# Hybrid decoder layer on one core: a third buffer for weights and their two parts, and the GLA diagonal moved into a score run

## The chip, the core and the metric

The kernel runs on one core of a Trainium2 chip. The metric is the device time of one execution in microseconds; the number given for a kernel is the median of its runs. Beside it there is a profile of one execution, taken by the hardware profiler. The engines of the core are TensorE (PE; its weight loads are PEld), VectorE (DVE), ScalarE (ACT), GpSimd (POOL) and SyncE (SP); SP, ACT and POOL also issue transfers (DMAs).

## The reference

One layer of a hybrid decoder over 16 meta tokens and 512 tokens (528 rows), width 2048, in float32. The normalised input goes through one projection of 7,585 columns; three token mixers share its columns, each on heads of its own; their outputs, gated, go through one output projection of 2048 x 2048, the input is added, and a last RMS norm follows.

```python
h = rms_norm(x, norm_w)
proj = h @ w_in
(dq, dk, dv, dz, db, da, gq, gk, gv, gz, gl, fq, fk, fv, fz, ff) = split_cols(proj)
...
o_dn = gated_delta_rule_chunked(q_dn, k_dn, v_dn, log_a, beta)      # 6 heads of 128
o_gla = gla_chunked(q, k, v, log_g)                                 # 5 heads, keys 64, values 128
o_fox = forgetting_attention(q, k, v, log_f)                        # 5 heads of 128
...
o = jnp.concatenate([o_dn, o_gla, o_fox], axis=-1)
return x + o @ w_out
```

The change touches the scores of GLA, linear attention with a decay for each key dimension. Within a chunk

```python
dec = jnp.exp(jnp.where(causal, g_c[:, :, :, None, :] - g_c[:, :, None, :, :], -jnp.inf))
attn = jnp.einsum('bhid,bhjd,bhijd->bhij', q_c, k_c, dec)
```

On the diagonal (i = j) the decay is 1, so the score there is the plain product of a token's query and its key.

## The kernel before

**Precision.** TensorE multiplies most operands as pairs: a float32 array is split into a high part, which ScalarE casts (`A.copy(hi, raw)`, L170), and a low part, the difference, which VectorE makes (L171). Each product then takes three matmuls: high by high, high by low, low by high.

**The weights.** A weight block is 128 columns of the input projection; its 2048 rows come as two halves of 128 x 1024 numbers (512 KB). `load_half` (L143) has SP load a half into a buffer `raw` (L147) and splits it into `whi` and `wlo`. The three kinds of buffer are tags (`raw`, `hi`, `lo`) of the pool `wp`, each with two buffers of 4 KB per partition. Where sums of weights are to be prepared, a copy from DRAM to DRAM (into `ti` or `tw`) is tied behind a raw load on SP's queue (L149), and POOL later adds to it by accumulating transfers (L490, L495). The split has high priority in the order of ScalarE and VectorE.

**The stages.** TensorE goes through the blocks in turn, with `inproj_part` (L238): two groups of 264 columns (all 528 rows) by 16 row tiles by 3, that is 96 matmuls a block, 48 a half; a block without meta tokens has 48 matmuls of 512 columns. First come four gate blocks (`dz`, L307) while the input itself arrives (`xs`, split into `xh` and `xl`) and ScalarE sums the squares of the token rows (`xt`, ten loads of up to 512 KB, L342 and L343, which go through the same tags `raw`, `hi` and `lo` in turn); then the delta-rule heads, the GLA gates, three GLA head pairs (heads 0 and 1, 2 and 3, and 4 alone), and the forgetting-attention heads, of which the later ones use pairs of blocks with seven products instead of eight (`inproj_pair`, L576: 24 matmuls a product). The output projection (L1426), with weights of 512 columns, and the last norm end the kernel.

**The order of the work.** The program is ordered ahead of time: each engine gets one list, from priorities and a simulated schedule. For single matmuls the place among those of the projection is written by hand: `PLACE` (L202) gives, for the first matmul into a named PSUM tile, a block and the number of that block's matmul behind which it shall stand. `"pss11": (('fv', 0), 26)` puts the first matmul of score run 1 of GLA pair 1 behind matmul 26 of block `fv` 0. A tile not in the table goes where the schedule puts it.

**GLA scores.** `gla_pair` (L981 on) computes the scores of a chunk by levels. For level s (64, 32, 16, 8, 4, 2, 1) the tokens are cut into blocks of 2s; queries of the second half of each block meet keys of the first half, both scaled by the decay to the boundary. VectorE subtracts (L1044, L1046), ScalarE takes the exponential (L1047), and VectorE scales keys and queries into `kq` (L1048, L1051). Two levels form a run, whose 64x64 matmuls (L1071, PSUM tiles `pss<pair><run>`, one per head) then stand together; a run's results are copied by ScalarE (levels 64 and 32) or by VectorE with a mask (`copy_predicated`, L1086) into `a64`, and from there by ScalarE into `at` (L1089), which the product with the values reads (`pgo`, L1139). Level 1 uses the unscaled keys.

The diagonal was done apart: POOL multiplies keys by queries (L1027), four matmuls per pair with a constant of two columns (`half_c`) sum over the key dimension of each head (`psd`, L1030), and VectorE spreads the column over the diagonal through a mask (L1032).

float32 operands that are not split take TensorE two instructions for each matmul in the profile, so a run of two levels and two heads shows as x64.

Of the kernel before, what the change touches and what calls it, by code (L numbers as in the profile page):

```python
# [8 lines left out]
F32 = mybir.dt.float32  # L9
F32R = mybir.dt.float32r  # L10
# [4 lines left out]
ALU = mybir.AluOpType  # L15
# [3 lines left out]
P = 128  # L19
D = 2048  # L20
KT = D // P
NM = 16
# [3 lines left out]
NB = S // P  # L26
# [56 lines left out]
def tile_hybrid_trunk(ctx, tc, xT, xtok, mtok, w_gate, w_in, w_out, w_dn, consts, lmask, fin_w, out, dbg=None):  # L83
    nc = tc.nc
# [3 lines left out]
    cst = pool("cst", 1)  # L88
    hp = pool("hp", 2 * KT)
    wp = pool("wp", 2)  # L90
# [3 lines left out]
    psm = pool("psm", 4, space=PSUM)  # L94
# [8 lines left out]
    V, A, G, PE = nc.vector, nc.scalar, nc.gpsimd, nc.tensor  # L103
# [10 lines left out]
    G.memset(ones, 1.0)  # L114
    eps_c = cst.tile([P, 1], F32, name="eps_c")
    G.memset(eps_c, EPS)
    half_c = cst.tile([P, 2], F32, name="half_c")
    G.memset(half_c, 0.0)
    for e in range(2):
        G.memset(half_c[64 * e : 64 * e + 64, e : e + 1], 1.0)  # L120
    zero_c = cst.tile([P, 1], F32, name="zero_c")
    G.memset(zero_c, 0.0)
    cpk = cst.tile([P, 101], F32, name="cpk")
# [19 lines left out]

    def load_half(src, name, raw=None):
        if raw is None:
            raw = wp.tile([P, 1024], F32, tag="raw", name=f"raw{name}")
        ring.append(nc.sync.dma_start(out=raw, in_=src).ins)  # L147
        if moves:
            x = nc.sync.dma_start(**moves.pop(0)).ins  # L149
            tc.add_manual_dep(x, ring[-1].name, mybir.DependencyInfo(  # L150
                mybir.DependencyClass.NoSync, mybir.DependencyReason.DATA), reason="ring")
            ring.append(x)
        hi = wp.tile([P, 1024], F32R, tag="hi", name=f"whi{name}")
        lo = wp.tile([P, 1024], F32R, tag="lo", name=f"wlo{name}")
        split(raw, hi, lo)
        due[0] += rate[0]
        while due[0] > 0 and chores:
            cost = next(chores[0], None)
            if cost is None:
                chores.pop(0)  # L160
            else:
                due[0] -= cost
        return hi, lo
# [34 lines left out]
    def part(name, n=512):  # L198
# [6 lines left out]
        "pss02": (('gk', 2), 26),  # L205
        "pss03": (('gk', 2), 46),
        "pg00": (('gk', 2), 72),
        "pss10": (('fk', 0), 92),
        "pss11": (('fv', 0), 26),
        "pss12": (('fv', 0), 54),  # L210
        "pss13": (('fv', 0), 78),
        "pg01": (('fq', 0), 8),
        "pss21": (('fk', 1), 60),
        "pss22": (('fk', 1), 84),
        "pgo2": (('pair', 0), 8),
    }

    def behind(mm, n):
# [118 lines left out]
    for b in range(5):  # L337
        r = NM if b == 4 else P
        for c in range(2):
            t = wp.tile([P, 1024], F32, tag=("raw", "hi", "lo")[(2 * b + c) % 3], name=f"xt{b}{c}")  # L340
            src = mtok if b == 4 else xtok[b * P : (b + 1) * P]
            nc.sync.dma_start(out=t[:r], in_=src[:, c * 1024 : (c + 1) * 1024])  # L342
            A.activation(t[:r], t[:r], AF.Square, accum_out=ssq[:r, b, c : c + 1])  # L343
# [11 lines left out]
    A.copy(rstd[:, :NM], pr[1][:, :NM])  # L355


    wgr = wp.tile([P, 1024], F32, tag="raw", name="rawgate")
    nc.sync.dma_start(out=wgr, in_=w_gate)
    wg = []  # L360
    for i, tag in enumerate(("hi", "lo")):
        w3 = wp.tile([P, 8, P], F32R, tag=tag, name=f"wg{i}")
        r3 = wgr[:, 512 * i : 512 * i + 512].rearrange("p (k c) -> p k c", c=64)
        A.copy(w3[:, :, 0:64], r3)
        V.tensor_tensor(out=w3[:, :, 64:], in0=r3, in1=w3[:, :, 0:64].bitcast(F32), op=ALU.subtract)
        wg.append(w3)
# [613 lines left out]
    def gla_pair(p):  # L980
# [41 lines left out]
        def masked(i, n):  # L1022
            return lmk[:, i, :].unsqueeze(1).to_broadcast([P, n, 64])


        prod = spare[:R]
        G.tensor_tensor(out=prod, in0=kT[:, NM:], in1=qT[:, NM:], op=ALU.mult)  # L1027
        psd = psm.tile([P, 512], F32, tag="m", name=f"psd{p}")
        for b in range(NB):
            PE.matmul(psd[:, b : b + NB * (ne - 1) + 1 : NB], prod[:, b * P : (b + 1) * P], half_c[:R, :ne],  # L1030
                      start=True, stop=True)
        V.copy_predicated(a64[:, :n_n], masked(5, n_n), psd[:, :n_n].unsqueeze(2).to_broadcast([P, n_n, 64]))  # L1032

        halves = lambda t_, s: t_.rearrange("p (n h s) -> p n h s", h=2, s=s)

        def scores(s, li):
# [14 lines left out]
            kqs.append(V.tensor_tensor(out=v4[:, :, 1, :], in0=qv[:, :, 1, :], in1=dv[:, :, 1, :], op=ALU.mult).ins)  # L1051
            return kq if s > 1 else kT[:, NM:], kq

        runs, li = ((64, 32), (16, 8), (4, 2), (1,)), 0
        for ri, run in enumerate(runs):
            ops = []
            for s in run:
                ops.append((s, *scores(s, li)))
                li += 1
            pss = [psm.tile([P, 512], F32, tag="m", name=f"pss{p}{ri}{e}") for e in range(ne)]  # L1060
            heads2 = [(e, pss[e], slice(64 * e, 64 * e + 64), slice(NB * e, NB * e + NB)) for e in range(ne)]
            c, got = 0, []
            for s, kx, qx in ops:
                n = s if s > 16 else 64
                for b in range(NB):
                    for r in range(P // (2 * n) if s > 16 else 2):
                        k0 = b * P + r * (2 * n if s > 16 else n)
                        q0 = k0 + n if s > 16 else k0
                        o0 = 2 * n * r if s > 16 else n * r
                        for e, ps, rr, en in heads2:  # L1070
                            mm = PE.matmul(ps[o0 : o0 + n, c + b * n : c + b * n + n], kx[rr, k0 : k0 + n],  # L1071
                                           qx[rr, q0 : q0 + n], start=True, stop=True)
                            place(f"pss{p}{ri}", mm)
                got.append((s, c, c + NB * n))
                c += NB * n
            for s, c0, c1 in got:
                for e, ps, rr, en in heads2:
                    pc = ps[:, c0:c1].rearrange("p (n c) -> p n c", n=NB)
                    if s == 64:
                        A.copy(at[0:64, en, 64:128], pc[0:64])  # L1080
                    elif s == 32:
                        for q in range(2):
                            sl = slice(64 * q, 64 * q + 32)
                            A.copy(a64[sl, en, 32:64], pc[sl])
                    else:
                        V.copy_predicated(a64[:, en], masked((16, 8, 4, 2, 1).index(s), NB), pc)  # L1086
        for q in range(2):
            sl = slice(64 * q, 64 * q + 64)
            A.copy(at[sl, :n_n, sl], a64[sl, :n_n])  # L1089
# [339 lines left out]
    halves = lambda w: [[t[:, j * 512 : (j + 1) * 512] for t in w] for j in range(2)]  # L1429

    def load_last(kp):
        raw = wp.tile([P, 1024], F32, tag="raw", name=f"rawl{kp}")
# [269 lines left out]
```

## Time and profile before

| | |
|---|---|
| median of 3 runs | 980.81 us (980.05 to 981.07) |
| the profiled execution: its time / its span | 981.26 us / 979.6 us |
| granted TensorE clock in it | 0.998 |
| TensorE / weight loads / VectorE / ScalarE / GpSimd busy | 967.9 / 890.6 / 674.9 / 477.0 / 229.7 us |
| transfers | 191.88 MB; SP's queue 152.63 MB, POOL's 31.66 MB |

The page gives, for each engine, the time in which it was busy, its share of the span and the number of instructions. A group of instructions is one line of the source, engine, operation and tiles, with the number of instructions, then busy time, mean length of one in ns, idle time of the engine just before them and what ended it. A wait reads "who <- for whom: us in total, times, longest". In a timeline each row has start, length, engine, line, operation, tiles written <- read, shape, count, and in brackets the idle time before. A table by stage gives for each stretch its length and then the busy time (and count) of PE, PEld, DVE, ACT and POOL, the granted clock, the share of the DMA engines and GB/s. Matmuls are pipelined: one is shown with its whole length, longer than the distance to the next.

### The profile page before, as it was taken

The numbers are of one execution on the slowest core, as the hardware profiler recorded it, in microseconds if no ns is written. First come the engines' busy times: TensorE is split into PE (matmuls) and PEld (weight loads), VectorE is DVE, ScalarE is ACT, GpSimd is POOL, SyncE is SP. The second block draws the span as 40 slices with busy tenths as digits, with TensorE's granted clock in tenths as the row PEclk, the third lists the DMA queues.
The fourth block names the chain that finished last, engine by engine and source line by source line (L and its number), as shares of the span: only waits on it lengthen the run. The fifth ranks groups of instructions, "written<-read, shape, count | busy, mean of one in ns | idle before, by whom it ended". The sixth has DMA issues, their size and how long they took to land.

```text
span 979.6 us, 19040 instructions
## 1 busy us (share of the span) xinstructions
PE 967.9 (99%) x7362; PEld 890.6 (91%) x7362; DVE 674.9 (69%) x1462; ACT 477.0 (49%) x1043; POOL 229.7 (23%) x251
## 2 busy tenths in 40 slices
PE   9999999999999999999999999999999999999996
PEld 7899999899999888899999889899999998888885
DVE  5468777876558885344685858766867768986664
ACT  7754433345356334344545545554555545544345
POOL 0032322232123234211213223232332120000023
PEclk9999999999999999999999999999999999999999
DMA  9835587987558787644647566678775478456534
GB/s 345 302 129 208 179 204 212 283 234 219 171 151 233 211 231 197 170 119 101 161 132 192 140 174 166 197 202 228 195 202 173 173 264 287 148 204 217 182 127 173
DMA packets 70336, 191.88 MB, mean 196 GB/s; under 512 B 14077, under 2 KB 17325, under 8 KB 69476
## 3 DMA queue, kind: packets, MB, share of 16 engines
q1 hardware_dynamic: 46048, 152.63, 44.7%
q0 software_dynamic: 15104, 31.66, 18.6%
q10 hardware_dynamic: 9092, 6.36, 2.3%
q8 instruction: 58, 0.95, 0.4%
q14 instruction: 34, 0.28, 0.1%
HBM read 179.93 MB, written 60.88 MB: 246 GB/s over the span
## 4 chain that ended last, share of the span: by engine, by line
PE 95%; DVE 2%; DMA 1%; issue 1%; ACT 0%; POOL 0%; SPq 0%; ACTq 0%; DVEq 0%
PE pp L238 46%; PE pp_a L576 8%; PE pq L1426 6%; PE pp L307 5%; PE pa L1426 3%; PE pt L1426 3%; PE ps L1426 3%; PE pp_b L576 2%; PE pp_d L576 2%; PE pp_c L576 2%; PE pr L1426 1%; PE pss L1071 1%; PE pfo L1301 1%; PE pgate L424 1%; DMA zd<-gqk 1%
## 5 line engine op out<-in xcount | busy, mean ns | idle before, releaser
L238 PE MATMUL pp<-xh,whi 128*128 128x264 f32 (+2 forms) x1120 | 270.3, 306 | 0.0
L238 PE MATMUL pp<-xh,wlo 128*128 128x264 f32 (+2 forms) x1120 | 268.9, 305 | 1.0 <-DVE wlo L171 1.0
L238 PE MATMUL pp<-xl,whi 128*128 128x264 f32 (+2 forms) x1120 | 269.7, 305 | 0.0
L170 ACT CAST whi<-raw 128x1024 fp32r<-128x1024 f32 x131 | 137.2, 1047 | 186.6 <-PE pp L238 115.4
L171 DVE TENSOR_TENSOR wlo<-raw,whi 128x1024 fp32r<-128x1024 f32 x131 | 162.3, 1239 | 53.3 <-ACT whi L170 46.4
L238 PEld LDWEIGHTS pp<-xh,wlo 128*128 128x128 f32 x1120 | 181.3, 189 | 9.5 <-DVE wlo L171 1.2
L238 PEld LDWEIGHTS pp<-xl,whi 128*128 128x128 f32 x1120 | 181.5, 189 | 8.8 <-issue 0.5
L238 PEld LDWEIGHTS pp<-xh,whi 128*128 128x128 f32 x1120 | 181.2, 188 | 8.8
L383 POOL TENSOR_SCALAR stc<-cv 128x528 f32<-128x528 f32 (+1 forms) x18 | 28.4, 1579 | 129.2 <-DVE cv L618 127.5
L618 DVE SCALAR_TENSOR_TENSOR cv<-pb,cpk,cv 128x528 f32<-128x528 f32 (+1 forms) x54 | 40.8, 756 | 0.8
L1455 POOL TENSOR_TENSOR acc<-acc,fw 128x512 f32<-128x512 f32 x4 | 6.1, 1552 | 138.4 <-DVE wll L171 138.4
L170 ACT CAST whis<-raws 128x1024 fp32r<-128x1024 f32 x20 | 20.7, 1049 | 28.2 <-PE pq L1426 12.2
L171 DVE TENSOR_TENSOR wlos<-raws,whis 128x1024 fp32r<-128x1024 f32 x20 | 24.2, 1223 | 14.9 <-ACT whis L170 14.8
L576 PE MATMUL pp_a<-t,whi 128*128 128x264 f32 (+1 forms) x224 | 29.3, 282 | 0.0
L576 PE MATMUL pp_a<-xl,whi 128*128 128x264 f32 x112 | 28.3, 287 | 0.0
L576 PE MATMUL pp_a<-xh,whi 128*128 128x264 f32 x112 | 28.1, 284 | 0.0
L576 PEld LDWEIGHTS pp_a<-t,whi 128*128 128x128 f32 x224 | 27.6, 188 | 0.0
L490 POOL DMA_DIRECT2D tw<-tw x16 | 13.4, 835 | 59.5 <-DVE wlo L171 30.2
L372 DVE TENSOR_TENSOR pb<-pp,rstd 128x264 f32<-128x264 f32 (+1 forms) x36 | 13.8, 424 | 19.5 <-PE pp L238 19.4
L383 POOL TENSOR_SCALAR stdz<-zdz 128x512 f32<-128x512 f32 x6 | 11.2, 1876 | 63.7 <-DVE zdz L401 55.3
L1426 PE MATMUL pq<-whia,a 128*128 128x512 f32 x80 | 25.5, 394 | 0.0
L1426 PE MATMUL pq<-whis,s 128*128 128x512 f32 x80 | 25.3, 394 | 0.0
(510 smaller groups left out, 2129.4 us busy)
## 6 DMA issues: line engine op xcount, KB each, us to landing
raw<-in_w_in SPq DMA_DIRECT2D x103, 512.0 KB, 3.9
ti<-in_w_in SPq DMA_DIRECT2D x28, 512.0 KB, 5.3
raw<-ti SPq DMA_DIRECT2D x28, 512.0 KB, 3.5
tw<-in_w_dn SPq DMA_DIRECT2D x20, 512.0 KB, 5.1
raws<-tw SPq DMA_DIRECT2D x15, 512.0 KB, 4.1
ti<-in_w_in POOLq DMA_DIRECT2D x14, 512.0 KB, 6.9
ti<-ti POOLq DMA_DIRECT2D x14, 512.0 KB, 6.5
tw<-in_w_dn POOLq DMA_DIRECT2D x10, 512.0 KB, 7.2
```

Of the source, the lines that this page charges most:

```text
L170: pace[0] = A.copy(hi, raw).ins
L171: pace[1] = V.tensor_tensor(out=lo, in0=raw, in1=hi.bitcast(F32), op=ALU.subtract).ins
L238: mm = PE.matmul(p_[:, :nt], wt[:, j * m : (j + 1) * m], xx[k][:, t0 : t0 + nt], start=(k == 0 and wt is hi and xx is xh), stop=(k == KT - ...
L307: mm = PE.matmul(ps[:, :S], wt[:, j * P : (j + 1) * P], xx[k][:, NM:T], start=(k == 0 and wt is hi and xx is xh), stop=(k == KT - 1 and wt ...
L372: V.tensor_tensor(out=o, in0=p_[rows], in1=rstd[rows, t0 : t0 + n], op=ALU.mult)
L383: maxes.append(G.tensor_scalar_max(t, src, LOW).ins)
L424: PE.matmul(pgate[a][:, :HT], wg[k // 8][:, k % 8, :], xx[k][:, a * HT : (a + 1) * HT], start=(k == 0 and xx is xh), stop=(k == KT - 1 and ...
L490: x = G.dma_start(out=out_[s], in_=in_[s], accum_op=ALU.add, max_dma_last_dim=2048)
L576: m = PE.matmul(p_[:, cols], wt[:, j * P : (j + 1) * P], xx[j][part_][:, cols], start=first and i == 0, stop=i == len(todo) - 1, skip_grou ...
L618: V.scalar_tensor_tensor(out=c, in0=pb[:, t0 + w : w + T], scalar=cwc[:, blk, w : w + 1], in1=c, op0=ALU.mult, op1=ALU.add)
L1071: mm = PE.matmul(ps[o0 : o0 + n, c + b * n : c + b * n + n], kx[rr, k0 : k0 + n], qx[rr, q0 : q0 + n], start=True, stop=True)
L1426: mm = PE.matmul(p_, o_[:, s], w_, start=(first and n == 0), stop=(last and n == 2), skip_group_check=True)
```

## The change

Four things change together.

1. The tags `raw`, `hi` and `lo` have three buffers each instead of two, for weights, the token rows, the gate weights and the last output weights alike.
2. The memory for that, 12 KB per partition, comes from the scratch of GpSimd's transfers: the program is built with 4,096 bytes per partition for it, where the default is 16,384.
3. The diagonal of the GLA scores is no longer computed apart. The last run of each pair, which held level 1 alone, gets a level 0: unscaled keys by unscaled queries in 64x64 blocks, one more half of the PSUM tiles that the run has; its results go through `copy_predicated` with the mask of the diagonal. The POOL product, `half_c` and the `psd` matmuls go.
4. In `PLACE` the score runs of pair 1 move back (run 0 from matmul 92 of `fk` 0 to matmul 4 of `fv` 0, which is 8 matmuls, run 1 by 12, run 2 by 6), run 0 and run 3 of pair 2 get a place, its runs 1 and 2 move back by 12 and 10, and its product with the values (`pgo2`) moves back by 16.

```diff
     def load_half(src, name, raw=None):
         if raw is None:
-            raw = wp.tile([P, 1024], F32, tag="raw", name=f"raw{name}")
+            raw = wp.tile([P, 1024], F32, tag="raw", bufs=3, name=f"raw{name}")
...
-        hi = wp.tile([P, 1024], F32R, tag="hi", name=f"whi{name}")
-        lo = wp.tile([P, 1024], F32R, tag="lo", name=f"wlo{name}")
+        hi = wp.tile([P, 1024], F32R, tag="hi", bufs=3, name=f"whi{name}")
+        lo = wp.tile([P, 1024], F32R, tag="lo", bufs=3, name=f"wlo{name}")
...
-        "pss10": (('fk', 0), 92),
-        "pss11": (('fv', 0), 26),
-        "pss12": (('fv', 0), 54),
+        "pss10": (('fv', 0), 4),
+        "pss11": (('fv', 0), 38),
+        "pss12": (('fv', 0), 60),
         "pss13": (('fv', 0), 78),
         "pg01": (('fq', 0), 8),
-        "pss21": (('fk', 1), 60),
-        "pss22": (('fk', 1), 84),
-        "pgo2": (('pair', 0), 8),
+        "pss20": (('fk', 1), 34),
+        "pss21": (('fk', 1), 72),
+        "pss22": (('fk', 1), 94),
+        "pss23": (('fq', 1), 10),
+        "pgo2": (('pair', 0), 24),
...
-            t = wp.tile([P, 1024], F32, tag=("raw", "hi", "lo")[(2 * b + c) % 3], name=f"xt{b}{c}")
+            t = wp.tile([P, 1024], F32, tag=("raw", "hi", "lo")[(2 * b + c) % 3], bufs=3, name=f"xt{b}{c}")
...
-        prod = spare[:R]
-        G.tensor_tensor(out=prod, in0=kT[:, NM:], in1=qT[:, NM:], op=ALU.mult)
-        psd = psm.tile([P, 512], F32, tag="m", name=f"psd{p}")
-        for b in range(NB):
-            PE.matmul(psd[:, b : b + NB * (ne - 1) + 1 : NB], prod[:, b * P : (b + 1) * P], half_c[:R, :ne],
-                      start=True, stop=True)
-        V.copy_predicated(a64[:, :n_n], masked(5, n_n), psd[:, :n_n].unsqueeze(2).to_broadcast([P, n_n, 64]))
...
-        runs, li = ((64, 32), (16, 8), (4, 2), (1,)), 0
+        runs, li = ((64, 32), (16, 8), (4, 2), (1, 0)), 0
...
-                ops.append((s, *scores(s, li)))
+                ops.append((s, *scores(s, li)) if s else (0, kT[:, NM:], qT[:, NM:]))
...
-                        V.copy_predicated(a64[:, en], masked((16, 8, 4, 2, 1).index(s), NB), pc)
+                        V.copy_predicated(a64[:, en], masked((16, 8, 4, 2, 1, 0).index(s), NB), pc)
...
-    nc = bacc.Bacc("TRN2", target_bir_lowering=False, num_devices=1)
+    nc = bacc.Bacc("TRN2", target_bir_lowering=False, num_devices=1, dynamic_dma_scratch_size=4096)
```

More of the change, by code (lines that the diff above doesn't have):

```diff
@@ L116, in tile_hybrid_trunk @@
     G.memset(eps_c, EPS)
[L117 to L120, printed above, removed]
     zero_c = cst.tile([P, 1], F32, name="zero_c")
@@ L355, in tile_hybrid_trunk @@
     A.copy(rstd[:, :NM], pr[1][:, :NM])
-    wgr = wp.tile([P, 1024], F32, tag="raw", name="rawgate")
+    wgr = wp.tile([P, 1024], F32, tag="raw", bufs=3, name="rawgate")
     nc.sync.dma_start(out=wgr, in_=w_gate)
@@ L361, in tile_hybrid_trunk @@
     for i, tag in enumerate(("hi", "lo")):
-        w3 = wp.tile([P, 8, P], F32R, tag=tag, name=f"wg{i}")
+        w3 = wp.tile([P, 8, P], F32R, tag=tag, bufs=3, name=f"wg{i}")
         r3 = wgr[:, 512 * i : 512 * i + 512].rearrange("p (k c) -> p k c", c=64)
@@ L1431, in load_last @@
     def load_last(kp):
-        raw = wp.tile([P, 1024], F32, tag="raw", name=f"rawl{kp}")
+        raw = wp.tile([P, 1024], F32, tag="raw", bufs=3, name=f"rawl{kp}")
         nc.sync.dma_start(out=raw, in_=w_out[3, kp])
```

## The prediction

> **What bounds the kernel now.** I read the head of the page first, then TensorE's waits, then the chain of waits in order of time (start, length, what).
>
> ```profile
> span 979.6 us, 19040 instructions
> PE 967.9 (99%) x7362; PEld 890.6 (91%) x7362; DVE 674.9 (69%) x1462; ACT 477.0 (49%) x1043; POOL 229.7 (23%) x251
> ...
> PE 95%; DVE 2%; DMA 1%; issue 1%; ACT 0%; POOL 0%; SPq 0%; ACTq 0%; DVEq 0%
> ```
>
> ```profile
> PE pss L1071 <- DVE kq L1051: 1.4, 2, 1.2
> PE warm L302 <- POOL ones L114: 1.2, 1, 1.2
> PE pp L238 <- DVE wlo L171: 1.0, 1, 1.0
> ```
>
> ```profile
> 563.00 1.09 PE pss L1071 x64
> ...
> 594.65 0.98 PE psd L1030 x8
> ...
> 612.80 1.08 PE pss L1071 x32
> ...
> 709.63 2.93 PE pp_a L576 x24
> ...
> 969.39 2.14 PE pz L1426 x18
> ```
>
> TensorE is busy for 967.9 of 979.6 us, so it is idle for 11.7. Its last matmul ends at 969.39 + 2.14 = 971.5, which leaves a tail of 8.1 us. The start takes 1.2 us, the wait for `ones`. The other 2.4 us are the two remaining rows of waits, 1.4 and 1.0. Between start and tail there is next to nothing to win from idle time; what is left is the number and the length of the matmuls. Their pace: 24 of 264 columns take 2.93 us, 0.122 us each.
>
> Where do those 2.4 us lie? The timeline of one stretch, TensorE and then VectorE (start, length, what, idle before and who ended it), and its table by stage answer that.
>
> ```profile
> 550.90 0.41 PE L238 MATMUL pp<-xl,whi 128*128 128x264 f32 x2
> 552.26 0.51 PE L238 MATMUL pp<-xh,wlo 128*128 128x264 f32 x2 [0.95 <-DVE wlo L171]
> 552.93 1.13 PE L1071 MATMUL pss<-kq 64*64 64x64 f32 x48 [0.16 <-DVE kq L1051]
> ```
> ```profile
> 558.62 0.29 PE L1071 MATMUL pss<-kq 64*64 64x64 f32 x4 [1.22 <-DVE kq L1051]
> ```
>
> ```profile
> 543.68 1.23 DVE L171 TENSOR_TENSOR wlo<-raw,whi 128x1024 fp32r<-128x1024 f32 x1 [3.78 <-ACT whi L170]
> ...
> 551.00 1.21 DVE L171 TENSOR_TENSOR wlo<-raw,whi 128x1024 fp32r<-128x1024 f32 x1
> ...
> 556.69 1.21 DVE L171 TENSOR_TENSOR wlo<-raw,whi 128x1024 fp32r<-128x1024 f32 x1
> ...
> 558.16 0.41 DVE L1051 TENSOR_TENSOR kq<-gqk,gvt 128x256 f32<-128x256 f32 x1
> ...
> 558.83 0.41 DVE L1051 TENSOR_TENSOR kq<-gqk,gpr 128x256 f32<-128x256 f32 x1
> ```
>
> ```profile
> 539.00:543.60 4.60, 4.60 (x39) 4.60 (x39) 0.74 (x1) 1.00 (x2) 0.00 (x0) 1.00 0.27 104
> 543.60:566.00 22.40, 20.07 (x306) 18.88 (x306) 22.20 (x50) 12.08 (x26) 5.78 (x4) 1.00 0.53 128
> ```
>
> This is the second GLA pair. The third busy time in the table's rows is VectorE's: 0.74 of 4.60 us, then 22.20 of 22.40. VectorE stands idle for 3.78 us until ScalarE has cast a high part, and right after that it is the bound: the low part that TensorE wants at 551.14 (two matmuls after 550.90) is made from 551.00 to 552.21, and the second score run wants its `kq`, of 558.57 and 559.24, at 557.2. Counted by starts TensorE loses 552.26 - 551.14 = 1.1 us, then 552.93 - 552.50 = 0.4, then 1.22 and some 0.16 that the end of the matmul before covers, 1.4: 2.9 us, a little more than the table's 2.4.
>
> **Part by part.** *The diagonal's own matmuls* go: 16 instructions for two pairs, 8 for the third.
>
> ```profile
> L1030 PE MATMUL psd<-half_c,gpr 128*128 128x2 f32 x16 | 1.9, 241 | 0.0
> L1071 PE MATMUL pss<-kq,gqk 64*64 64x64 f32 x80 | 2.0, 223 | 0.0
> ```
> ```profile
> L1032 DVE COPY_PREDICATED kq<-lmk,psd 128x512 f32<-128x512 uint8 x2 | 1.5, 744 | 0.3 <-PE psd L1030 0.3
> L1086 DVE COPY_PREDICATED kq<-lmk,pss 128x256 f32<-128x256 uint8 x25 | 9.7, 441 | 3.6 <-PE pss L1071 3.5
> ```
>
> TensorE saves 1.9 + 0.98 = 2.9 us. Instead the last score run of each pair gets a level 0, keys by queries without decay, as large as level 1, whose row is the one with `kq,gqk`: 80 instructions. By the chain's runs, 64 instructions of a pair with two heads take 1.09 us, so two pairs pay 2 x 32 x 1.09/64 = 1.1; with one head 32 take 1.08, so 16 cost 0.5. (The group's 2.0 counts the pipeline's length at the ends of three runs; as the other bound it makes 2.0 of the 1.6.) Net: -2.9 + 1.6 = **-1.3 us**, at worst -0.9, all on the path, since TensorE hardly idles.
>
> VectorE loses two masked copies of 744 ns and a third of half the width (441 by the other row), and gains five of 441: 2.2 for 1.9, nothing either way. The new ones stand behind those of level 1, so ScalarE's copies of `a64` into `at`, which wait for all of them, come 0.4 to 0.9 us later. Queued behind these on ScalarE are casts of the next weights, now a buffer ahead; TensorE's product of scores and values waits for `at`. In the third pair:
>
> ```profile
> 627.63 0.81 ACT L1089 COPY kq<-kq 64x256 f32<-64x256 f32 x2
> ```
> ```profile
> 631.48 0.89 PE pgo L1139 x8
> ```
>
> There are 3 us between the two, and the change puts that product a further 16 matmuls (2 us) back. So the delay is hidden; uncovered it would cost this pair, with one head, 0.4 us. POOL loses three products and three memsets; it is 23% busy, and none of TensorE's waits but that for `ones` names it: nothing.
>
> *The third buffers.* SP's queue can start a raw load one half block earlier (48 matmuls, 5.9 us), and ScalarE and VectorE can split it as much earlier. No transfer and no split is added; the copies between DRAM tensors and the stores behind a raw load on SP's queue move forward with it. In the stretch above the low part of 551.00 moves into the idle 3.78 us, and TensorE's 1.1 us goes. Late next is `kq`, since VectorE must still do the rest of its 22.20 us in order.
>
> *The later places.* In the second pair run 0 goes 8 matmuls back, run 1 12, run 2 6; run 3 stays. Without its stalls TensorE would come to run 1 at 558.62 - 2.9 = 555.7, and now 12 x 0.122 = 1.5 us later, at 557.2. The first `kq` is ready at 558.57 today: sooner by one split, 1.21 us, if all of the lead shows up here, and no sooner if another split (that of 556.69 or a later one) slides into the place. That is a wait of 0.2 to 1.4 us; I take 0.8, the middle, as no row tells the two apart. Run 2 then follows 0.8 + 1.1 + 22 x 0.122 later, at 561.8, 1.2 before the 563.00 of today; VectorE's lead covers just that. So of 2.9 us of stalls **2.1** go (1.5 to 2.7). The third pair has no wait in the table, so its later places gain nothing; they cost nothing either, because behind them stand only its own products, whose output goes to DRAM until the output projection. The first pair keeps its places.
>
> *The scratch* concerns only transfers that POOL issues:
>
> ```profile
> L490 POOL DMA_DIRECT2D tw<-tw x16 | 13.4, 835 | 59.5 <-DVE wlo L171 30.2 <-DVE fsm L1264 12.8 <-DVE fm L1265 5.9
> ```
>
> An issue takes 835 ns, and the idle time before it is put down to VectorE, not to a lack of room. I take nothing; the other end stands with the rivals.
>
> Sum: 1.3 + 2.1 = **3.4 us** off the profiled execution's 981.26 (its span of 979.6 and 1.7 around it): 977.9. The median shown, 980.81, is 0.45 below that execution, so in medians **977.4 us**. With the bounds 0.9 + 1.5 = 2.4 to 1.3 + 2.7 = 4.0 come off: 978.4 to 976.8. About 0.2% (2 us) is what a measurement of this kernel can tell from no change.
>
> **Rivals.** *VectorE stays the bound.* Its full stretch of 22.4 us is longer than the lead of 5.9 us that a buffer gives. If the low parts take their places ahead of `kq` as before, the 1.1 us for `wlo` goes, but `kq` is no earlier, and TensorE, which now comes sooner, waits that much longer at runs 0 to 2. Only the arithmetic stays: 980.81 - 1.3 = 979.5, no measurable change. For it: 22.20 of 22.40. Against it: runs 0 and 1 stand 1.0 and 1.5 us later, about as long as their waits, and VectorE has 3.78 us free just before.
>
> *The first stage becomes slower* (the other sign). The token rows `xt` use the same buffers ahead of the weights, and nine are then free instead of six.
>
> ```profile
> 19.19 2.22 SPq L342 DMA_DIRECT2D xt<-in_xtok  x3
> 22.39 0.64 SPq L273 DMA_DIRECT2D xs<-in_xT  x1
> 23.93 0.33 SPq L186 DMA_DIRECT2D raw3q<-in_w_in  x1
> 24.61 0.33 SPq L342 DMA_DIRECT2D xt<-in_xtok  x1
> ```
> ```profile
> 30.16 1.06 ACT L343 ACTIVATE xt<-xt 128x1024 f32<-128x1024 f32 x1
> ...
> 32.18 0.62 ACT L170 CAST w3q<-raw3q 128x512 fp32r<-128x512 f32 x1
> ```
> ```profile
> 33.92 0.39 PE L307 MATMUL pp<-xh,w3q 128*128 128x512 f32 x1
> ```
>
> The seventh `xt` goes at 24.61 today. If three more are issued right behind those of 19.19, the `xs` of 22.39 and the quarter of 23.93 come behind 3 x 512 KB more. By the issues alone (2.22 us for three) that is 2.2 us; at the 345 GB/s of the first slice it is 4.6:
>
> ```profile
> GB/s 345 302 129 208 179 204 212 283 234 219 171 151 233 211 231 197 170 119 101 161 132 192 140 174 166 197 202 228 195 202 173 173 264 287 148 204 217 182 127 173
> ```
>
> ScalarE would also square three more rows ahead of them, 3 x 1.06 = 3.2 us. It has the quarter cast at 32.80 and TensorE wants it at 33.92, so 1.1 us are free. The loss is 2.2 + 3.2 - 1.1 = 4.3 to 4.6 + 3.2 - 1.1 = 6.7 us: 981.7 to 984.1. The kernel is slower than before from 3.4 us of loss on, measurably from 5.4; a delay below 1.1 shows nothing. Against it: the three loads in a row of today cost TensorE no wait, and ScalarE may take them up after the casts.
>
> *POOL waits for room in its scratch.* If one of its issues waited for an earlier transfer to land, 7.2 us by this row, what is queued behind it on POOL (the maxima ahead of each SiLU, the masks of the heads) would be as late.
>
> ```profile
> tw<-in_w_dn POOLq DMA_DIRECT2D x10, 512.0 KB, 7.2
> ```
>
> Where other work covers it, it costs nothing; one such wait uncovered gives 977.4 + 7.2 = 984.6. Against it: POOL is idle for 77% of the span. [...]
>
> *Much more than forecast.* If the 99% of TensorE hid stalls, deeper buffers could remove them, at most the time without a weight load: 979.6 - 890.6 = 89 us, which would give 892. [...] The trace does not bear that out here:
>
> ```profile
> PEld 7899999899999888899999889899999998888885
> ```
>
> the slices of 24.5 us below nine are mostly the start, 320 to 415 us and all from 810 us on, stages with matmuls of 512 columns, where a load is shorter than its matmul, or the stretch above; and 264 columns take 0.122 us at 709 as at 550.
>
> **How the numbers follow.** Forecast 0.66; VectorE stays the bound 0.17; the first stage 0.08; POOL's scratch 0.04; much more 0.02; an order of the instructions that costs 2 us and more elsewhere 0.03. Forecast and much more lie below 978.8, faster by over 0.2%: 0.68. The same: VectorE as the bound, and 0.03 of the two that lose time, where they lose only what the rest gains: 0.20. Slower: the remaining 0.12. The range takes in the forecast's bounds, 1.8 us below them for waits too short for the table (it shows a wait only beyond the 0.16 us that the matmul before covers), the second case and the lower end of the first stage's: 975.0 to 982.0, which leaves out some 0.14.
>
> **What would show it.** In the profile after: no `psd` rows and 80 more instructions at the scores' line; `pp <- wlo` gone from TensorE's waits, `kq` there with about 0.8 us; TensorE busy some 1.3 us less; VectorE's idle 3.78 us before the second pair's scores filled with a low part. I am wrong if TensorE waits in the first 50 us, if `kq` waits for more than 1.5 us, or if POOL's issues grow past 1 us.

## The result, and the profile after

The kernel with the change takes 998.17 us in the median of 4 runs (995.96 to 998.43), the kernel before 980.94 us (4 runs) beside it: 17.2 us more, a ratio of 1.0169 [1.0157, 1.0181]. The forecast was 977.4. The profiled execution took 995.96 us, 14.7 more than that of before (span 994.3 against 979.6); it is the fastest of the four, so the profile accounts for 14.7 of the 17.2 us. Line numbers from here on are those of the changed kernel, some 2 to 10 lower (scores L1061, `kq` L1041, low parts L167); rows of the kernel before and of the runs below carry the numbers of their own kernel.

The head of the page after (busy times, the slices of TensorE and of its granted clock):

```profile
span 994.3 us, 19170 instructions
PE 971.5 (98%) x7418; PEld 891.9 (90%) x7418; DVE 671.5 (68%) x1464; ACT 477.8 (48%) x1043; POOL 226.3 (23%) x245
...
PE   9999999999999999999999999999999999699996
...
PEclk9999999999999999999999999999999999799998
```

TensorE was idle for 994.3 - 971.5 = 22.8 us, against 11.7 before: 11.1 more. It was busy for 3.6 us more, although it had less to do. Those two make the 14.7. Slice 35 (845 to 870 us) holds the most of both, a 6 in TensorE's row and a 7 in the clock's. TensorE's waits say for what:

```profile
PE pfw L1283 <- DVE fm L1256: 5.6, 1, 5.6
PE pss L1061 <- DVE kq L1041: 3.5, 2, 2.4
PE pfx L1261 <- DVE fp L1258: 2.1, 1, 2.1
PE warm L300 <- POOL ones L114: 1.2, 1, 1.2
PE pfx L1261 <- DVE fm L1256: 1.1, 1, 1.1
PE pp L305 <- ACT xh L293: 0.8, 1, 0.8
PE pq L1416 <- DVE wloa L167: 0.5, 1, 0.5
PE pp_a L574 <- ACT vf L592: 0.5, 1, 0.5
```

The wait for `wlo` is gone, as foretold. In its place stand seven rows that the kernel before did not have, or had smaller, and the largest is in the forgetting attention, which the change does not touch. Two of the three signs of being wrong that the prediction named are among them, a wait in the first 50 us (`xh`, at 40.8 us) and `kq` for more than 1.5 us.

**The end.** `pfx` transposes the probabilities of the last block of the last attention head, and `pfw` the head's probabilities for the meta tokens; VectorE makes both in a chain of small instructions: two maxima (L1247, L1249), the sign (L1252), ScalarE's exponential, the reciprocal (L1254), two scalings (L1255, L1258), a low part (L1256). VectorE's timeline before, and then after:

```profile
829.87 0.56 DVE L1257 CUSTOM_DVE_ANT_0 fp<-pfa,fqk 128x400 f32<-128x400 f32 x1
...
832.77 0.23 DVE L1266 SCALAR_TENSOR_TENSOR fm<-fp,fsm,fm 128x16 fp32r<-128x16 f32 x1
...
839.65 1.76 DVE L643 TENSOR_TENSOR zr<-zr 128x256 f32<-128x256 f32 x5
```

```profile
842.33 0.56 DVE L1247 CUSTOM_DVE_ANT_0 fp<-pfa,fqk 128x400 f32<-128x400 f32 x1
...
843.42 1.76 DVE L641 TENSOR_TENSOR zr<-zr 128x256 f32<-128x256 f32 x5
...
849.32 0.14 DVE L1252 TENSOR_SCALAR fsm<-fsm 128x1 f32<-128x1 f32 x1
...
854.00 0.15 DVE L1254 RECIPROCAL fsm<-fsm 128x1 f32<-128x1 f32 x1
...
855.74 2.76 DVE L627 TENSOR_TENSOR s<-zr,s 128x256 fp32r<-128x256 f32 x8
858.42 0.22 DVE L1255 TENSOR_SCALAR fm<-fp,fsm 128x16 fp32r<-128x16 f32 x1
...
865.35 0.22 DVE L1256 SCALAR_TENSOR_TENSOR fm<-fp,fsm,fm 128x16 fp32r<-128x16 f32 x1
```

Before, the chain took from 829.87 to 833.00, 3.1 us, and the output projection's sums (`zr`, `s`) began 6.7 us later. After, the first five sums come between the first maximum and the second, and sums, low parts and accumulations stand between all further links but the two scalings: from 842.33 to 865.57 it is 23.2 us. VectorE is not slower, it is busy for all of these 23.2 us; it does its instructions in another order, in which the small ones that TensorE waits for come last. TensorE's timeline at that place:

```profile
859.17 0.98 PE L1261 MATMUL pfx<-ident,fp 128*128 128x128 f32 x4 [2.07 <-DVE fp L1258]
865.72 0.45 PE L1283 MATMUL pfw<-ident,fm 128*128 128x128 f32 x1 [5.57 <-DVE fm L1256]
```

**The third GLA pair.** The wait of 2.4 us for `kq` lies at 616 us. The timeline before, then after:

```profile
613.53 0.52 ACT L553 ACTIVATE xe<-xe,cpk 128x264 f32<-128x264 f32 x1 [2.94 <-DMA xe<-in_xT]
...
613.80 0.51 PE L238 MATMUL pp<-xh,whi 128*128 128x512 f32 x1
...
614.94 0.41 DVE L1051 TENSOR_TENSOR kq<-gqk,gvt 64x256 f32<-64x256 f32 x1
...
616.09 0.62 PE L1071 MATMUL pss<-kq 64*64 64x64 f32 x14
```

```profile
612.95 0.68 PE L1061 MATMUL pss<-kq 64*64 64x64 f32 x16
614.06 0.51 ACT L551 ACTIVATE xe<-xe,cpk 128x264 f32<-128x264 f32 x1 [4.64 <-DMA xe<-in_xT]
...
615.13 0.42 DVE L1038 TENSOR_TENSOR kq<-gqk,gvt 64x256 f32<-64x256 f32 x1 [3.38 <-ACT gvt L1037]
...
616.03 0.68 PE L1061 MATMUL pss<-kq 64*64 64x64 f32 x16 [2.40 <-DVE kq L1041]
```

In both kernels ScalarE waits for a transfer of the next stage's input (`xe`, a multiplication that stands ahead of the exponential on ScalarE's list), and the exponential, and so `kq`, come after it. Before, nine projection matmuls stood between the second run's scores and the next, from 613.80 until those at 616.09, and `kq` was ready at 615.35 (614.94 + 0.41): covered, with 0.7 us to spare. After, the next scores are due at once, at 613.6, and `kq` is ready at 615.88. The order of the matmuls here changed as well, and with it the cover was gone.

**Half pace.** TensorE's matmuls after that wait, and a table by stage for the end:

```profile
618.26 0.63 PE L236 MATMUL pp<-xh,wlo 128*128 128x512 f32 x1
618.68 0.63 PE L236 MATMUL pp<-xh,whi 128*128 128x512 f32 x1
...
620.39 0.39 PE L236 MATMUL pp<-xl,whi 128*128 128x512 f32 x1
620.62 0.40 PE L236 MATMUL pp<-xh,wlo 128*128 128x512 f32 x1
```

```profile
865.70:869.50 3.80, 3.78 (x10) 3.03 (x11) 0.34 (x1) 1.21 (x5) 0.00 (x0) 0.50 0.39 139
869.50:874.00 4.50, 4.50 (x24) 3.89 (x23) 1.60 (x2) 1.93 (x3) 0.00 (x0) 0.99 0.00 0
```

From 617.0 to 620.4 (granted clock 0.50) the matmuls of 512 columns follow each other every 0.42 us, then every 0.23; after the wait of 5.57 us the granted clock is 0.50 for 3.8 us. 3.4 us and 3.8 us at half pace lose 1.7 and 1.9 us, and that is why TensorE's busy time rose by 3.6 with less to do. With the 1.3 us that the diagonal should save, 1.3 us of the busy time stay without a place; the four transposes at 859.17, which take 0.98 us against 0.60 before, are 0.4 of them.

### The profile page after: what moved, and what is told of

Read it like the earlier page. It is cut to its first block, busy times and chain, and to the rows that moved or that the text cites. A ratio compares the mean times of both kernels' runs of the same rounds, so it can differ in the third digit from the quotient of the medians.

```text
span 994.3 us, 19170 instructions
## 1 busy us (share of the span) xinstructions
PE 971.5 (98%) x7418; PEld 891.9 (90%) x7418; DVE 671.5 (68%) x1464; ACT 477.8 (48%) x1043; POOL 226.3 (23%) x245
## 4 chain that ended last, share of the span: by engine, by line
PE 83%; DMA 5%; DVE 5%; issue 4%; ACT 1%; POOL 1%; SPq 0%; ACTq 0%; POOLq 0%; DVEq 0%
PE pp L236 42%; PE pp_a L574 7%; PE pq L1416 4%; PE pa L1416 3%; PE pt L1416 3%; PE ps L1416 3%; PE pp_b L574 2%; PE pp_c L574 2%; DMA xt<-in_xtok 2%; PE pp_d L574 2%; PE pr L1416 2%; PE pp L305 1%; DMA zd<-gqk 1%; PE pfo L1291 1%; PE pgate L422 1%
## 5 line engine op out<-in xcount | busy, mean ns | idle before, releaser
L167 DVE TENSOR_TENSOR wlo<-raw,whi 128x1024 fp32r<-128x1024 f32 x131 | 161.5, 1233 | 48.1 <-ACT whi L166 41.5
L616 DVE SCALAR_TENSOR_TENSOR cv<-pb,cpk,cv 128x528 f32<-128x528 f32 (+1 forms) x54 | 40.8, 756 | 0.9
L167 DVE TENSOR_TENSOR wlos<-raws,whis 128x1024 fp32r<-128x1024 f32 x20 | 24.0, 1221 | 10.8 <-ACT whis L166 10.6
L488 POOL DMA_DIRECT2D tw<-tw x16 | 13.4, 835 | 63.0 <-DVE wlo L167 33.8
L166 ACT CAST whia<-rawa 128x1024 fp32r<-128x1024 f32 x15 | 15.4, 1049 | 23.9 <-PE pq L1416 9.0
```

The costliest lines, as they stand in the source:

```text
L166: pace[0] = A.copy(hi, raw).ins
L167: pace[1] = V.tensor_tensor(out=lo, in0=raw, in1=hi.bitcast(F32), op=ALU.subtract).ins
L488: x = G.dma_start(out=out_[s], in_=in_[s], accum_op=ALU.add, max_dma_last_dim=2048)
L616: V.scalar_tensor_tensor(out=c, in0=pb[:, t0 + w : w + T], scalar=cwc[:, blk, w : w + 1], in1=c, op0=ALU.mult, op1=ALU.add)
```

## The experiments

Four theories. A: the three buffers let low parts and the next stage's sums go ahead of the last attention block on VectorE, and this order costs the time. B: third buffers cost by themselves. C: the small scratch. D: the later places of the score runs, or the larger last run. The diffs of the runs that leave parts of the change away stand against the changed kernel, those of single parts against the kernel before. `add_manual_dep` puts one instruction behind another on the same engine's list and adds no work.

**Three buffers alone** (with the scratch that pays for them; no diagonal, no places).

```diff
-            raw = wp.tile([P, 1024], F32, tag="raw", name=f"raw{name}")
+            raw = wp.tile([P, 1024], F32, tag="raw", bufs=3, name=f"raw{name}")
...
-    nc = bacc.Bacc("TRN2", target_bir_lowering=False, num_devices=1)
+    nc = bacc.Bacc("TRN2", target_bir_lowering=False, num_devices=1, dynamic_dma_scratch_size=4096)
```

> Three buffers and the small scratch, the diagonal and the places as before. Theory A (the third buffer lets low parts and the next stage's sums go ahead of the last attention block on VectorE, so TensorE waits some 8 us there and runs slowly for 3 us after): by the list of VectorE's instructions the sums stand behind that block here, so TensorE's waits there should be under 1 us and the time 978 to 984 us. Rival B (the third buffers by themselves cost the time, through transfers and low parts that crowd others): 993 to 999 us, waits of the same size in the profile. Rival C (the small scratch costs it): 993 us or more, with longer issues on GpSimd.

982.22 us, ratio 1.0016 [1.0003, 1.0029]. TensorE's two waits for `kq`, the first in the second pair, the other in the third, and one table row behind the longer of them:

```profile
553.02 1.13 PE L1071 MATMUL pss<-kq 64*64 64x64 f32 x48 [1.10 <-DVE kq L1051]
...
619.38 0.68 PE L1071 MATMUL pss<-kq 64*64 64x64 f32 x16 [1.57 <-DVE kq L1051]
```

```profile
620.30:623.50 3.20, 3.20 (x26) 2.54 (x24) 3.17 (x12) 2.70 (x8) 1.25 (x2) 0.61 0.13 49
```

No wait at `pfw` or `pfx`. B falls as the cause of the 17 us. In the second pair the buffers do what the prediction leant on: the wait for `wlo` goes, and 1.1 us of waiting is left of 2.4. But the third pair, which had no wait, now has one of 1.6 us with a slow clock behind it (0.61 over 3.2 us), and together that is a small loss.

**The rest without the buffers** (diagonal and places, two buffers, default scratch).

```diff
-            raw = wp.tile([P, 1024], F32, tag="raw", bufs=3, name=f"raw{name}")
+            raw = wp.tile([P, 1024], F32, tag="raw", name=f"raw{name}")
...
-    nc = bacc.Bacc("TRN2", target_bir_lowering=False, num_devices=1, dynamic_dma_scratch_size=4096)
+    nc = bacc.Bacc("TRN2", target_bir_lowering=False, num_devices=1)
```

> The diagonal in the score run and the later places, but two buffers and the scratch of before. Theory A: the sums stand behind the last attention block, no long wait there; TensorE has 1.3 us less work, and runs 0 and 1 of the second pair wait less: 977 to 981 us. Rival D (the later places and the larger last run cost the time, by making the heads that follow late): 990 us or more, with TensorE's waits for kq above 3 us.

979.96 us, ratio 0.9995 [0.9985, 1.0006]. TensorE busy 965.9 us. Its stretch of the second pair, by stage:

```profile
539.00:543.60 4.60, 4.60 (x41) 4.60 (x40) 3.04 (x5) 3.30 (x6) 1.35 (x2) 1.00 0.37 110
543.60:566.00 22.40, 22.40 (x386) 21.50 (x385) 21.31 (x51) 11.43 (x25) 5.26 (x4) 1.00 0.54 133
```

TensorE is busy for 22.40 of 22.40 us, where it had 20.07 before, and VectorE's free time just before is filled (3.04 of 4.60 us, against 0.74). That is with two buffers, so the third was not needed for it. This profile is of the fastest of the ten runs (978.39); it has one wait for `kq` of 0.9 us, in the third pair.

**The scratch alone.**

```diff
-    nc = bacc.Bacc("TRN2", target_bir_lowering=False, num_devices=1)
+    nc = bacc.Bacc("TRN2", target_bir_lowering=False, num_devices=1, dynamic_dma_scratch_size=4096)
```

> The kernel before with 4,096 bytes for GpSimd's transfers and nothing else. Theory A: no difference, 980 to 982 us, GpSimd's issues 0.8 to 1.0 us each. Rival C: issues that wait for room, 985 us or more.

980.69 us, ratio 1.0000 [0.9991, 1.0010]. C falls.

**The change with the sums held** behind the last low part of the last attention block, on VectorE.

```diff
-            V.tensor_tensor(out=lo[:, :n, bs], in0=x, in1=hi[:, :n, bs].bitcast(F32), op=ALU.subtract)
+            attended[:] = [V.tensor_tensor(out=lo[:, :n, bs], in0=x, in1=hi[:, :n, bs].bitcast(F32), op=ALU.subtract).ins]
...
+            for x in two:
+                tc.add_manual_dep(x.ins, attended[0].name, ...)
```

> The changed kernel with one order more: on VectorE the first sums for the output projection stand behind the last low part of the last attention block. Nothing is computed differently. Theory A: TensorE's waits for fp and fm of the last head (2.1 and 5.6 us) and the slow clock behind them (some 2 us) go, the 2.4 us wait for kq of the third pair and its slow clock stay: 986 to 990 us. Rivals B, C and D: the sums' place is a symptom, the wait goes to another step: 994 us or more.

986.09 us, ratio 1.0060 [1.0042, 1.0079]: 12.1 us less than the change. Its waits:

```profile
PE pss L1066 <- DVE kq L1046: 3.5, 3, 1.9
...
PE pfx L1266 <- DVE fm L1261: 1.1, 1, 1.1
PE pp L305 <- ACT xh L293: 1.1, 1, 1.1
```

Those of 5.6 and 2.1 are gone, and no work was added or taken away (`two` are the first sums, L641 and L642). That shows the second half of A, that this order costs the time, for 12 of the 17 us; what brings the order about comes below. In the profiled spans it is 994.3 - 984.0 = 10.3 us: 7.7 of waiting, 1.9 of half pace behind it, and small differences.

**The change without the diagonal** (three buffers, scratch, later places).

```diff
-        runs, li = ((64, 32), (16, 8), (4, 2), (1, 0)), 0
+        runs, li = ((64, 32), (16, 8), (4, 2), (1,)), 0
...
+        psd = psm.tile([P, 512], F32, tag="m", name=f"psd{p}")
```

> The change without its diagonal part: three buffers, the small scratch and the later places of the score runs, with the diagonal scores computed as before. By the instruction list the last attention head's last block then stands unbroken on VectorE, ahead of the output projection's sums. Theory A (the broken block on VectorE is what costs): no TensorE waits of over 1 us at pfw or pfx, 980 to 983 us, near the 982.2 of the three buffers alone. Theory D (the later places of the score runs cost): 990 us and more, since the places are those of the change. Either way the wait for kq in the third GLA pair may stay, at 1 to 3 us.

980.93 us, ratio 1.0004 [0.9990, 1.0018], no wait at `pfw` or `pfx`; one of 1.9 us for `kq` in the third pair. D falls for the places.

**The change with the old places.**

```diff
-        "pss10": (('fv', 0), 4),
+        "pss10": (('fk', 0), 92),
...
-        "pgo2": (('pair', 0), 24),
+        "pgo2": (('pair', 0), 8),
```

> The change with the places of its score runs put back to those of before: three buffers, the small scratch and the diagonal in the last score run stay, and the block of the last attention head is broken up on VectorE as in the change. Theory A: 994 to 1000 us, with the waits at pfw and pfx of 5 and 2 us still there. Theory D (the later places cost): 980 to 987 us, those waits gone.

996.16 us, ratio 1.0158 [1.0139, 1.0177]. Its first three rows of waits:

```profile
PE pfw L1281 <- DVE fm L1254: 5.9, 1, 5.9
PE pss L1059 <- DVE kq L1039: 4.1, 3, 2.1
PE pfx L1259 <- DVE fp L1256: 2.1, 1, 2.1
```

The damage is there with the old places, and not there with three buffers alone, with the buffers and the places, or with the diagonal and two buffers. Only three buffers and the level 0 together tip the order. Why the planner then puts the sums first was not settled.

**xe held as well:** the multiplications of the next stage's input behind the last exponential of the third pair, on ScalarE, added to the kernel with the sums held.

```diff
-            A.activation(x12, x12, AF.Copy, scale=nwc[:, k : k + 1])
+            y = A.activation(x12, x12, AF.Copy, scale=nwc[:, k : k + 1])
+            tc.add_manual_dep(y.ins, exps[-1].name, ...)
...
-                A.activation(d, d, AF.Exp, scale=SC)
+                exps.append(A.activation(d, d, AF.Exp, scale=SC).ins)
```

> The change with the block of the last attention head kept whole (as in the run before, 986.1 us) and, in addition, ScalarE's multiplications of the next stage's input (xe) held behind the last exponential of the third GLA pair. If ScalarE's wait for the DMA of xe is what makes the exponential, kq and so TensorE late at 616 us: that wait of 2 to 2.6 us goes, 983 to 984 us, 2 to 3 us less than the run before. If VectorE itself is late there: no change, 986 us, and a wait of 2 us or more for kq in the third pair.

982.74 us, ratio 1.0021 [1.0010, 1.0033], 3.3 us less. The exponential now starts at 611.73, ahead of the first multiplication of `xe` (614.62), and the wait of 1.9 us in the third pair is gone: ScalarE's wait for `xe` was what made `kq` late there. The 2.1 us for `kq` that are left, in two waits of which none is over 1.3, are in the second pair.

**xt held as well:** the seventh and later loads of token rows behind the last load of `xs`, on SP's queue. In the change the seventh went ahead of the weight quarter `raw3q`, and the last three ahead of the last two loads of `xs` (SP's issues in the profile of the change):

```profile
24.50 0.33 SPq L340 DMA_DIRECT2D xt<-in_xtok  x1
25.23 0.33 SPq L182 DMA_DIRECT2D raw3q<-in_w_in  x1
26.47 0.33 SPq L340 DMA_DIRECT2D xt<-in_xtok  x1
27.15 1.64 SPq L340 DMA_DIRECT2D xt<-in_mtok  x2
29.71 1.68 SPq L271 DMA_DIRECT2D xs<-in_xT  x2
```

```diff
+            lastx[:] = [nc.sync.dma_start(out=xs[c], in_=xT[:, 2 * c : 2 * c + 2, :]).ins]
...
-            nc.sync.dma_start(out=t[:r], in_=src[:, c * 1024 : (c + 1) * 1024])
+            y = nc.sync.dma_start(out=t[:r], in_=src[:, c * 1024 : (c + 1) * 1024])
+            if 2 * b + c > 5:
+                tc.add_manual_dep(y.ins, lastx[0].name, ...)
```

> The kernel of the run before, and in addition the seventh and later loads of token rows (xt) held on SyncE's queue behind the last load of xs, as their buffers made them wait before the change. If the wait for xh of 0.8 to 1.1 us at 41 us comes from these loads going first: it goes, and 1 us comes off (982 to 983 us). If not: the wait stays and the time is the same as that of the run before within 0.5 us.

981.24 us, ratio 1.0001 [0.9991, 1.0010], 1.5 us less where 1 was expected, and no wait for `xh` (0.5 us in the profile of the run before). With the order mended in three places, all of the change is back at the time of before, but not below it.

**The best version: two buffers, diagonal, later places, xe held** (the edit of the second run and that of the hold, together).

> The diagonal in the last score run and the later places with two buffers each, as in the run of 979.96 us, and the multiplications of the next stage's input (xe) held behind the last exponential of the third GLA pair. That run's profile had one TensorE wait of 0.9 us for kq, in the third pair. If the same wait of ScalarE for xe made it: gone, and about 1 us below that run, 978.5 to 979.5, 0.1 to 0.2% below the kernel before. If not, 980 and the wait stays. The prediction's own sum for the whole change (977.4) is the lower end for what these two parts can give.

977.25 us, ratio 0.9964 [0.9950, 0.9977]: 3.8 us less than before and 21 less than the change. More was gained than the wait of 0.9 us that was to go. The profile, of the slowest of the five runs (979.13), has no wait in the third pair, but 1.2 (`wlo`) and 0.6 us (`kq`) in the second, where the same kernel without the hold had none.

**The diagonal alone** (two buffers, old places, old scratch).

```diff
-        runs, li = ((64, 32), (16, 8), (4, 2), (1,)), 0
+        runs, li = ((64, 32), (16, 8), (4, 2), (1, 0)), 0
```

> The diagonal in the last score run alone: two buffers each, the scratch and the places of before. If the prediction's term for the diagonal is right (1.3 us less of TensorE's time) and the waits of the second GLA pair stay as they are: 979 to 980 us, TensorE busy some 1 to 2 us less than 967.9. If the waits for wlo and kq (2.4 us in the profile of before) go through this part and not through the later places: 977 to 978.5. If the larger last score run makes a later kq the bound: 981 and more, with a wait of 2 us or more for kq.

980.49 us, ratio 1.0001 [0.9991, 1.0011]. TensorE is busy for 966.7 us, 1.2 less than before; `wlo` and `kq` are still waited for (0.8 and 1.7 us; 0.6 of the latter in the third pair).

**xe held alone, and the diagonal with xe held,** to see what is worth what in the best version (the hold's edit in the kernel before, and in that of the diagonal alone).

> The kernel before with one thing added: the multiplications of the next stage's input (xe) held behind the last exponential of the third GLA pair. No part of the change is in it. The kernel before has no TensorE wait in the third pair, so if the hold only helps by taking such a wait away: 981, no change. If the hold itself is worth something (the run of 977.25 had 2.1 us of waits left and is yet faster than its sum says): 978 to 979.5.

> The diagonal in the last score run and the hold of xe, with the places, the buffers and the scratch of before: the run of 977.25 us without the later places. If the later places are worth the 2.1 us that the prediction gave them: 979 to 980.5, 2 to 3 us above that run. If they are worth nothing: 977 to 978.5.

981.21 us, ratio 1.0004 [0.9995, 1.0013], and 978.47 us, ratio 0.9975 [0.9965, 0.9984]. The hold is worth nothing by itself, and the diagonal's gain comes out only with it. The two profiles with the diagonal, without the hold and with it, are 978.8 and 977.4 us long; the 1.4 us between them are as much as the wait of 0.6 in the third pair and that of 0.8 for `wlo` in the second, which are both gone. In the single runs of the diagonal alone the granted clock goes down to 0.994 to 0.997 in the five that took over 981 us; with the hold no run is below 0.997. A wait that differs from run to run, in the slower ones with a slow clock behind it as behind the 1.57 us above (0.61 over 3.2 us), would fit that; no profile shows such a run. The later places add 1.2 us (977.25 against 978.47, which is inside what was expected if they are worth nothing), but the two intervals overlap, so that this is not settled.

## Why the prediction was wrong

**The step that failed:** "No transfer and no split is added; the copies between DRAM tensors and the stores behind a raw load on SP's queue move forward with it." In the sum every stage that the change does not touch stands at nothing. I moved single instructions earlier in a list that otherwise stayed as it was. But the lists are made by a planner from simulated times. Other times gave other lists, on VectorE at the end, on TensorE in the third pair, on SP in the first stage, and what lost was work that the change does not touch. It was on paper as "an order of the instructions that costs 2 us and more elsewhere", with a chance of 0.03 and neither a place nor a price. A place and the start of a price stood in the profile of before: the chain of small VectorE instructions in the last attention block is 3.1 us long, the sums begin 6.7 us behind it, and TensorE takes up `fp` at 837.43, 4.6 us after it is ready (832.86), so that TensorE pays for whatever delays the chain by more. That the planner would put the sums first could not be read there. The runs put 12.1 us on that place, 3.3 on the third pair and 1.5 on the first stage; 12.1 + 3.3 + 1.5 = 16.9 of 17.2 (by the ratios, each with the kernel before beside it, 10.7, 3.8 and 2.0).

**The second failure:** "The third pair has no wait in the table, so its later places gain nothing; they cost nothing either". The places were indeed not to blame (with the old ones the third pair has a wait of 2.1 us), but the missing wait was read as slack. It was 0.7 us of slack behind nine matmuls. Besides, the price of a wait was taken to be its length; behind those of 2.40 and 5.57 us in the change stood 3.4 and 3.8 us at a granted clock of 0.50, by which 1.7 and 1.9 us more were lost.

**The diagonal:** the term was -1.3 us on TensorE; alone it measured 1.2 less busy time. No `psd` is left, and 56 instructions more are 80 at the scores' line less 24. With `xe` held it is 2.4 us of time, of which the second pair gave some 1.1: its profile has one wait of 1.1 us there, where `wlo` and `kq` took 2.2 before.

**The third buffers and the later places:** in the second pair they did what was foretold. The wait for `wlo` went, VectorE was busy for 4.11 of the 4.60 us in which it had been for 0.74, and TensorE waited for `kq` once, 1.1 us at run 1, where the prediction had 0.8 (0.2 to 1.4). The rival "VectorE stays the bound" was not borne out: with the buffers alone TensorE waits 1.1 us in this pair instead of 2.4, and the loss is in the third. But the lead of a buffer was not what it took: two buffers, with the diagonal and the later places, had no wait in that stretch. And the waits there come and go with every new order, 1.8 us of them when `xe` is held as well.

**The scratch:** nothing, as forecast. With 4,096 bytes and nothing else changed the ratio is 1.0000 [0.9991, 1.0010]; the issues at L490 take 824 ns in the median before, and the same ones in the change, which has 4,096 too, 824 as well (L488). Whether that room was ever full no run shows.

**The first stage:** the rival came true in kind, `xt` ahead of a weight quarter, at 0.5 to 1.1 us of wait and 1.5 us of time instead of 4.3 to 6.7. One load passed the quarter, not three; three passed the last `xs`.

**What stays open:** the three-buffer kernel with all holds is 4 us above the best version; its profile has 1.2 us (`pfx`) and 0.5 us (`pp_a`) of waits that the other lacks, and 0.7 instead of 1.8 us for `kq` and `wlo`. That does not make 4 us; but the two profiled spans, 978.4 and 977.4, are only 1.0 us apart, so that these profiles cannot show the rest. And that the best version, at 977.25, lies next to the forecast of 977.4 is chance: it lacks the third buffers, and the sum knew of no hold.

## What to carry to other kernels

Where a planner makes the instruction lists, a change of buffers or tiles can re-order stages that it does not touch: look in the profile of before for short chains whose result a saturated engine uses soon after, and price each with the work that could get ahead of it. A row without a wait is not a row with slack; subtract the ready time from the use time before you count on it. When a re-ordering costs, tie the one instruction behind the other before you give up the change, and measure each part without the others, since here one part's gain (2.4 us) showed only when an instruction of another stage was held back.

## What the runs showed of the hardware

Behind some waits of TensorE the granted clock was about half for a few microseconds. In the change, after the wait of 2.40 us that ends at 616.03, it was 0.50 from about 617.0 to 620.4. It was 0.50 again from about 859.3, just behind the wait of 2.07 us that ends at 859.17, to about 869.6, and the wait of 5.57 us lies inside that stretch. With the old places it was 0.50 as soon as the wait of 2.14 us ended at 617.44, and the matmuls of 512 columns followed each other every 0.43 us until 623.3; behind that run's wait of 2.07 us at `pfx` it was 1.00 over 0.9 us, and 0.50 by 864, inside the wait of 5.91 us that follows. By the table by stage, the wait of 1.88 us without the diagonal was followed by a clock of 0.60 over 3.3 us, the one of 1.57 us of the buffers alone by 0.61 over 3.2 (each began late), and one of 1.92 us by 0.51 over 3.2. Behind waits of 1.09 us (the change), 1.22 (before) and 1.28 us the clock was 1.00 over 3 us. Two such rows, after a wait of 1.28 us and after the one of 1.92 us, both of the kernel with the sums held:

```profile
560.00:563.00 3.00, 3.00 (x49) 2.79 (x43) 2.88 (x9) 2.08 (x4) 0.00 (x0) 1.00 0.52 187
...
617.30:620.50 3.20, 3.20 (x8) 2.50 (x8) 3.20 (x8) 0.79 (x2) 0.00 (x0) 0.51 0.38 106
```

So of these waits the three of up to 1.28 us had no such stretch behind them, and those of 1.57 us and more had one, but for the 2.07 us with the old places; 3.4 us of it, as after the wait of 2.40 us, cost 1.7 us on top of the wait. No run was made to vary the length of a wait, so neither a limit nor the cause is shown. The mean granted clock of a run, 0.989 to 0.991 in the four of the change against 0.996 to 0.999 before, shows it at a glance.

The same product of 64x512 numbers on GpSimd, with the same operands, took 4.38 us in the change and 1.51 before. What made it longer no run shows. In the change VectorE's small products follow each other without a gap meanwhile, until one of 0.41 us takes 1.50:

```profile
604.96 4.38 POOL L1085 TENSOR_TENSOR gt<-gt,gqk 64x512 f32<-64x512 f32 x1 [0.98 <-ACT gt L1084]
...
608.12 1.50 DVE L1038 TENSOR_TENSOR kq<-gqk,gvt 64x256 f32<-64x256 f32 x1
```

The first transfer of `xe` behind it starts only 0.4 us later than before (609.29 against 608.87, where it waited for VectorE), the second 1.7 us (612.52 against 610.85). At another place of the change a VectorE instruction of 128x16 numbers, 0.23 us in the median of its twenty, takes 3.84 us and ends at 708.58, when the last of three GpSimd instructions that follow each other from 705.16 on has ended as well (708.54):

```profile
704.74 3.84 DVE L1255 TENSOR_SCALAR fm<-fp,fsm 128x16 fp32r<-128x16 f32 x1
```

Before, one GpSimd instruction of 1.33 us stood beside it, and it took 1.35. Right behind the long one comes TensorE's wait of 1.1 us for `fm` at `pfx`; all five profiles with three buffers and the level 0 have such a wait, of 1.1 to 1.2 us. At both places the long instruction of one engine stands beside instructions of the other; whether that makes it long no run tried.
